# Where the weight-sum transfers of a two-layer hybrid transformer start, and which result each of them follows

## The chip, the cores and the metric

The kernel runs on one core of a Trainium2 chip. The metric is device time in microseconds (us) from launch to end, the median of several executions. The engines of a core work side by side, each through its own instructions in order: PE (TensorE) multiplies matrices, DVE (VectorE), ACT (ScalarE) and POOL (GpSimd) work on elements, SP (SyncE) does nothing here but issue DMA transfers. POOL issues some DMAs too. An instruction waits until what it reads has been written and what it overwrites has been read.

## The reference

Two layers of a transformer for 512 tokens of width 1024, in float32. Each layer is a half feed-forward network (width 2816), a token mix and another half feed-forward network, each with a residual and a layer norm:

```python
for l in range(DEPTH):
    x = _layer_norm(DN_ALPHA * x + 0.5 * _swiglu(x, ffn1_w1[l], ffn1_w2[l]), ln1_g[l], ln1_b[l])
    mix = _token_mix(x, w_in[l], ...)
    x = _layer_norm(DN_ALPHA * x + mix, ln2_g[l], ln2_b[l])
    x = _layer_norm(DN_ALPHA * x + 0.5 * _swiglu(x, ffn2_w1[l], ffn2_w2[l]), ln3_g[l], ln3_b[l])
```

The token mix projects the tokens with `w_in`, runs three kinds of attention over the parts, and merges them with gates:

```python
q_a, kv_a, g_a, q_b, k_b, v_b, q_c, k_c, v_c, f_c = _split_cols(h @ w_in)
o_a = _nsa(...)        # compressed, selected and windowed attention
o_b = _swa_sink(...)   # sliding window with sinks
o_c = _fox(...)        # attention with forget gates
g = jax.nn.sigmoid(h @ w_gate + b_gate).reshape(B, S, N_BRANCH, D)
merged = g[:, :, 0] * (o_a @ w_br_a) + g[:, :, 1] * (o_b @ w_br_b) + g[:, :, 2] * (o_c @ w_br_c)
return merged @ w_out
```

The first attention's compressed branch makes its keys and values by a small network over blocks of 32 tokens: `gelu(flat @ w1) @ w2`, with `cmp_k_w1`, `cmp_v_w1` (2048 x 256 each) as its first layer.

## The kernel before

**Matmuls.** Every large product is made of three matmuls of a reduced float type: a weight tile `raw` (128x1024, 512 KB) is loaded by SP, ACT rounds it to `hi` (L154), DVE makes `lo` = raw - hi (L155), and PE multiplies `hi` by the tokens' high and low part and `lo` by the high part (L175 to L177). `raw`, `hi` and `lo` have three buffers each, so the split of a tile waits until the tile three before it has been used by all that read it.

**The token mix** (`mix`) begins with 30 *chunks* (L1153 on), each a projection of 128 columns, split into 8 parts that are put between pieces of the attention. The chunks' weights are `w_in`, and `w_gate` for the last five. Among the first chunks PE also runs the cumulated forget gates (`cum`, L789 and L792) and, between parts, 16 steps of the compressed branch's first layer (`hid`, L842), whose weights are the 16 pairs of loads `cw` (L835, one pair for keys and values, 256 KB together). The `cw` tiles share the tag "p" and its 13 buffers with probabilities and other things, the `gl` tile of the forget gates among them, which `cum` reads. Behind the first layer comes `tr` (L855), run within the thirteenth chunk. Probabilities are normed (L915) on DVE or POOL and transposed by PE.

Behind the chunks comes the branches' part: for each of eight `d`, three gates (L1377 on; the result is `t`, with four buffers), the branch products `brp` with `oh` and `ol` (the split attention outputs, L1393 and L1394), and their sum `mh`. The branches' weights are `raw` of 256 KB each (L1371).

**Sums of weights.** The second layer of three of the four feed-forward networks is computed from sums of blocks of its weights (`ts`, in DRAM). They are made by DMA alone: `weight_sums` (L384) puts 24 steps for one weight into a queue, in three groups of eight. Each step is one transfer of 768 KB from DRAM to DRAM, issued by POOL (L396). Steps 3, 5, 6 and 7 of a group add onto what is there; steps 6 and 7 add sums onto sums (`ts<-ts`), and step 7 waits for step 6 to have landed. Layer 0 of `mix` has two weights to sum (48 steps), layer 1 has one (24). In all 72 steps.

One step is taken at the end of each chunk (L1167) and of each gate's matmuls (L1384), by `sums_step` (L402): POOL first copies one column of the `hi` tile that this chunk or gate uses to `pace`, then issues the transfer. The copy holds the transfer until that `hi` has been made, and it makes the copy one of the readers of `hi`.

**What sets the order.** PE and POOL run in the order in which the program is written; ACT, DVE and SP are ordered by a scheduler at build time.

Of the kernel before, what the change touches and what calls it, by code (L numbers as in the profile page):

```python
# [9 lines left out]
F32 = mybir.dt.float32  # L10
F32R = mybir.dt.float32r
BF = mybir.dt.bfloat16
AF = mybir.ActivationFunctionType
# [5 lines left out]
P = 128  # L19
S, D, F = 512, 1024, 2816  # L20
KD, KF, NB = D // P, F // P, S // P
# [43 lines left out]
def body(tc, a, out, depth=DEPTH):  # L65
    nc = tc.nc
    PE, POOL = mybir.EngineType.PE, mybir.EngineType.Pool

    def pool(name, bufs=1, side=None, **kw):
        return tc.alloc_tile_pool(name=name, bufs=bufs, side=side, **kw)  # L70

    const = pool("const")
# [8 lines left out]
    def ps(tag=None, name="ps", shape=(P, 512)):  # L81
        if tag is None:
            tag = PS_ALL[ring[0] % 8]
            ring[0] += 1
        return psp.tile(list(shape), F32, name=name, tag=tag, bufs=PS_TAGS[tag])
# [16 lines left out]
    bgate = const.tile([P, depth, 3, KD], F32, name="bgate")  # L102
    peT = const.tile([P, depth, 2, 32], F32, name="peT")
    stats = [const.tile([P, 8], F32, name=f"st{i}") for i in range(NB)]
    pace = const.tile([P, 48], F32, name="pace")[:, 0:1]

    xh = xtp.tile([P, KD, S], F32R, name="xh")
    xl = xtp.tile([P, KD, S], F32R, name="xl")
# [49 lines left out]
    def wcols(w, c0, step=None):  # L158

        r = wraw()  # L160
        nc.sync.dma_start(r, w.rearrange("(k p) f -> p k f", p=P)[:, :, c0:c0 + P])
        return wsplit(r, step=step)
# [16 lines left out]
    def proj(o, w, n=slice(0, S), ks=range(KD)):  # L179
        for k in ks:  # L180
            mm3(o[:, n], w, k, xh[:, k, n], xl[:, k, n], k == 0, k == KD - 1)
# [200 lines left out]
    sums = deque()  # L382
# [16 lines left out]
            sums.extend(lambda g=g, i=i: step(g, i) for i in range(8))  # L399
        return ts  # L400

    def sums_step(w, n=1):  # L402
        for _ in range(n):
            if sums:
                nc.gpsimd.tensor_copy(pace, w[0][:, KD - 1, 0:1].bitcast(F32))
                sums.popleft()()

    PLAIN = (0, 1, 2, 3)

# [245 lines left out]

    def mix(l, wts, pend, done_ffn, xap, xa, nxt):
        m = K()
        PB = 13
        w_in = a["w_in"][l]
        wb = [a["w_br_a"][l], a["w_br_b"][l], a["w_br_c"][l]]  # L660
# [91 lines left out]
        def ev_gf(p):  # L752
# [3 lines left out]
            def rest():  # L756
                pt = ps("tp", "gfT", (P, NB, 64))
                for tb in range(NB):
                    nc.tensor.transpose(pt[:, tb], t[0:64, tb * P:(tb + 1) * P], ident[0:64, 0:64])
                w = at.tile([P, 11, NB, H], F32, name="gl", tag="p", bufs=PB)  # L760
                gs = w[:, 0:4].rearrange("p a b h -> p (a b h)").rearrange("p (b c) -> p b c", b=NB)
# [41 lines left out]
        def ev_z(p, i):  # L803

            z = [at.tile([P, 8, 2, NSLOT], F32, name="z", tag="p", bufs=PB) for _ in range(2)]
            nc.gpsimd.memset(z[1][:, :, :, NSLOT - 1:NSLOT], 0.0)
# [13 lines left out]
        def conv(ws):  # L820


            c = K()
            w2 = at.tile([P, 2, 3, DH], F32, name="cw2", tag="p", bufs=PB)
            c.wk, c.wv = w2[:, :, 0:2], w2[:, :, 2]
            v = a["cmp_k_w2"][l].rearrange("(c p) d -> p c d", p=P)
            for r in range(2):
                nc.sync.dma_start(c.wk[:, :, r], v)
            nc.sync.dma_start(c.wv, a["cmp_v_w2"][l].rearrange("(c p) d -> p c d", p=P))
            wv = [w.rearrange("(c p) f -> p c f", p=P) for w in ws]  # L830

            def load(k):
                r = at.tile([P, 2, 256], F32, name="cw1", tag="p", bufs=PB)
                for i in range(2):
                    nc.sync.dma_start(r[:, i], wv[i][:, k])  # L835

                def go():
                    if k == 0:
                        c.p = ps("sc", "hid", (P, 256))
                    for i in range(2):  # L840
                        z = (m.zk, m.zv)[i][k // 8][:, k % 8].rearrange("p g n -> p (g n)")
                        nc.tensor.matmul(c.p[64 * i:64 * i + 64], z, r[:, i], start=k == 0, stop=k == 15)  # L842
                    if k == 15:
                        x = at.tile([P, 2, 256], F32, name="gl", tag="p", bufs=PB)
                        t, c.t = x[:, 0], x[:, 1]
                        nc.scalar.activation(t, c.p, AF.Square)
                        nc.vector.tensor_scalar(t, t, 0.044715, 1.0, op0=OP.mult, op1=OP.add)
                        nc.vector.tensor_tensor(t, t, c.p, op=OP.mult)
                        nc.scalar.activation(t, t, AF.Tanh, scale=GELU_C)
                        nc.vector.scalar_tensor_tensor(c.t, t, 1.0, c.p, op0=OP.add, op1=OP.mult)  # L850
                return go

            def tr():
                pt = ps("tp", "glT", (P, 2, P))
                for f in range(2):  # L855
                    nc.tensor.transpose(pt[:, f], c.t[:, f * P:(f + 1) * P], ident)
                x = at.tile([P, 3, P], F32, name="glt", tag="p", bufs=PB)
                c.gk = x[:, 0].rearrange("p (f n) -> p f n", f=2)
                c.gv = x[:, 1:3].rearrange("p f (g r n) -> p f g r n", g=2, r=2)
                nc.vector.tensor_copy(c.gk, pt[:, :, 0:64])  # L860
                for f in range(2):
                    nc.vector.tensor_copy(c.gv[:, f], pt[:, f, 64:P].rearrange("p (g n) -> p g n", g=2)[:, :, None]
                                          .to_broadcast([P, 2, 2, NSLOT]))

            c.n = 0

            def feed():

                if c.n < 16 and len(narrow) < 4:
                    narrow.append(load(c.n))  # L870
                    c.n += 1

            def end():
                while narrow or c.n < 16:
                    feed()
                    narrow.popleft()()
                tr()

            return c, feed, end
# [37 lines left out]
        class Swa:  # L917
            br, nseg, ngrp = 1, 1, 1
# [53 lines left out]
        class Fox:  # L972
            br, nseg, ngrp = 2, 2, 2
# [48 lines left out]
        class Nsa:  # L1022
            br, nseg = 0, 2
# [132 lines left out]
        def chunk(c0, then, w=w_in, load=wcols, bank="mm"):  # L1156
            st = K()

            def part(i):
                def go():  # L1160
                    if i == 0:
                        st.w = load(w, c0)
                        st.p = ps(bank, "pj")
                    proj(st.p, st.w, ks=range(i, i + 1))
                    if i == 7:
                        then(st.p)
                        sums_step(st.w)  # L1167
                return go

            fill.extend(part(i) for i in range(8))  # L1170
# [101 lines left out]
        def gate_ev(t, p, br, d):  # L1272
            nc.scalar.activation(t, p, AF.Tanh, scale=0.5, bias=bg[:, br, d:d + 1])
# [94 lines left out]
        def wbr(d, brs):  # L1368
            r = wraw()
            for j, br in enumerate(brs):  # L1370
                nc.sync.dma_start(r[:, 4 * j:4 * j + 4],  # L1371
                                  wb[br].rearrange("(k p) f -> p k f", p=P)[:, :, d * P:(d + 1) * P])
            return wsplit(r[:, 0:4 * len(brs)], 4 * len(brs))

        def gates(d):
            g_t = []
            for br in range(3):  # L1377
                if d == 1 and br < 2:
                    p = held[br]
                else:  # L1380
                    p = ps("sc" if d == 1 else None, "gate")
                    w = wcols(a["w_gate"][l], br * D + d * P)
                    proj(p, w)
                    sums_step(w)  # L1384
                t = tp_.tile([P, S], F32, name="t", tag="t", bufs=4)
                gate_ev(t, p, br, d)
                g_t.append(t)
            return g_t

        g_1 = gates(1)  # L1390
        for br in (1, 2, 0):
            for i in range(4):
                nc.scalar.activation(oh[br][i], o_t[br][i], AF.Copy)  # L1393
                nc.vector.tensor_tensor(ol[br][i], o_t[br][i], oh[br][i].bitcast(F32), op=OP.subtract)  # L1394
        for d in range(KD):
            g_t = gates0 if d == 0 else g_1 if d == 1 else gates(d)
            for br in (1, 2, 0):
                if br != 2:
                    w = wbr(d, (1, 2) if br else (0,))
                k0 = 4 if br == 2 else 0  # L1400
                p = ps(name="brp")
                for k in range(4):
                    mm3(p, w, k0 + k, oh[br][k], ol[br][k], k == 0, k == 3)
                t = g_t[br]
                nc.vector.scalar_tensor_tensor(t, t, 1.0, p, op0=OP.add, op1=OP.mult)
                if br != 1:
                    nc.vector.tensor_tensor(g_t[1], g_t[1], t, op=OP.add)
            nc.scalar.activation(mh[:, d], g_t[1], AF.Copy)
            nc.vector.tensor_tensor(ml[:, d], g_t[1], mh[:, d].bitcast(F32), op=OP.subtract)
# [147 lines left out]
```

## Time and profile before

| | us |
|---|---|
| median of the runs shown | 2498.09 |
| those three runs | 2498.33, 2498.09, 2495.55 |
| the profiled execution | 2495.75 |
| its span (first to last instruction) | 2494.0 |
| mean granted clock of PE | 0.993 |

| DMA issue | count | KB each | us to landing, median |
|---|---|---|---|
| `raw<-in_w_in_dram` | 56 | 512 | 5.0 |
| `raw<-in_w_gate_dram` | 48 | 512 | 5.3 |
| `ts<-in_ffn_w_dram` (steps 0 to 5) | 54 | 768 | 7.9 |
| `ts<-ts` (steps 6 and 7) | 18 | 768 | 8.8 |

A row of a timeline has the start in us, the duration (of several alike: the stretch), the engine and line, the operation with output and inputs, the count, and in brackets the idle time of that engine before it with what ended it. "SPq" and "POOLq" are rows of an engine's queue, DMA issues above all. A row of a table of stretches has the stretch, its length, the busy time of PE, PE's weight loads, DVE, ACT and POOL with the number of their instructions, and at its end the granted clock, the DMA engines' mean busy share and GB/s. The names in the rows are those of the program; `cw` is `cw1` in the code.

### The profile page before, as it was taken

How to read it: one execution, taken by the hardware profiler on the slowest of the kernel's cores; microseconds unless marked ns; L12 is line 12 of the kernel's file. 1: busy time of each engine (PE TensorE's matmuls, PEld its weight loads, DVE VectorE, ACT ScalarE, POOL GpSimd, SP SyncE). 2: the span in 40 equal slices, each digit the busy share in tenths (PEclk: the TensorE clock that was granted, in tenths of full speed). 3: DMA queues.
4: the chain of work that ended last, by engine and by line, in shares of the span. 5: the costliest groups of instructions: out<-in, count | busy, mean ns of one | idle time of the engine just before them, and what ended most of it. 6: DMA issues, size and time to landing. Idle time of an engine off the chain costs nothing. (4 is left out here: it accounts for less than half of the span.)

```text
span 2494.0 us, 40924 instructions
## 1 busy us (share of the span) xinstructions
PE 2443.8 (98%) x15529; PEld 2159.3 (87%) x15529; DVE 1763.2 (71%) x3554; ACT 1172.6 (47%) x2226; POOL 325.6 (13%) x598
## 2 busy tenths in 40 slices
PE   9999999899999999999999999979999999999998
PEld 8999887688878889999889998867888888899987
DVE  7888365477754367998879889655776543698887
ACT  4444334466642333445534446434766422344453
POOL 4000001234422100000000000112443000000000
PEclk9999999899999999999999999999999999999999
DMA  7445345885578642336623346668662433333463
GB/s 205 113 118 161 119 111 166 225 179 147 127 193 224 156 143 86 103 111 207 203 93 103 109 155 204 194 152 227 157 149 60 144 90 121 119 94 102 132 211 127
DMA packets 411460, 364.05 MB, mean 146 GB/s; under 512 B 19720, under 2 KB 351640, under 8 KB 411264
## 3 DMA queue, kind: packets, MB, share of 16 engines
q1 hardware_dynamic: 381968, 279.92, 38.0%
q0 software_dynamic: 29296, 81.53, 13.6%
q8 instruction: 122, 2.00, 0.3%
q14 instruction: 74, 0.61, 0.1%
HBM read 334.07 MB, written 74.51 MB: 164 GB/s over the span
## 5 line engine op out<-in xcount | busy, mean ns | idle before, releaser
L155 DVE TENSOR_TENSOR lo<-raw,hi 128x1024 fp32r<-128x1024 f32 (+2 forms) x384 | 450.5, 1182 | 379.3 <-ACT hi L154 374.5
L154 ACT ACTIVATE hi<-raw 128x1024 fp32r<-128x1024 f32 (+2 forms) x384 | 390.6, 1024 | 600.2 <-issue 149.9
L175 PE MATMUL pj<-xh,hi 128*128 128x512 f32 (+1 forms) x720 | 267.6, 372 | 0.2 <-ACT hi L154 0.2
L176 PE MATMUL pj<-xl,hi 128*128 128x512 f32 (+1 forms) x720 | 255.5, 355 | 1.1 <-DVE xl L241 1.1
L177 PE MATMUL pj<-xh,lo 128*128 128x512 f32 (+1 forms) x720 | 255.1, 354 | 0.0
L515 PE MATMUL pg<-xh,hi 128*128 128x256 f32 x864 | 245.1, 284 | 1.7 <-ACT sn L522 1.5
L515 PE MATMUL pg<-xh,lo 128*128 128x256 f32 x864 | 244.5, 283 | 0.0
L515 PE MATMUL pg<-xl,hi 128*128 128x256 f32 x864 | 244.5, 283 | 0.0
L435 ACT ACTIVATE hi<-ws 128x1024 fp32r<-128x1024 f32 x144 | 151.5, 1055 | 160.2 <-DVE ws L427 72.7
L436 DVE TENSOR_TENSOR lo<-ws,hi 128x1024 fp32r<-128x1024 f32 x144 | 175.4, 1220 | 17.6 <-ACT hi L435 17.4
L274 PE MATMUL acc<-hi,sh 128*128 128x512 f32 x450 | 175.5, 390 | 0.0
L274 PE MATMUL acc<-lo,sh 128*128 128x512 f32 x450 | 175.1, 389 | 0.0
L274 PE MATMUL acc<-hi,sl 128*128 128x512 f32 x450 | 175.1, 389 | 0.0
L515 PEld LDWEIGHTS pg<-xh,hi 128*128 128x128 f32 x864 | 165.8, 192 | 3.1 <-ACT sn L522 2.9
L515 PEld LDWEIGHTS pg<-xl,hi 128*128 128x128 f32 x864 | 165.8, 192 | 0.2
L515 PEld LDWEIGHTS pg<-xh,lo 128*128 128x128 f32 x864 | 165.8, 192 | 0.0
L515 PE MATMUL pu<-th,hi 128*128 128x256 f32 x576 | 163.0, 283 | 0.0
L515 PE MATMUL pu<-tl,hi 128*128 128x256 f32 x576 | 163.0, 283 | 0.0
L515 PE MATMUL pu<-th,lo 128*128 128x256 f32 x576 | 163.0, 283 | 0.0
L177 PEld LDWEIGHTS pj<-xh,lo 128*128 128x128 f32 x720 | 136.7, 190 | 19.8
L175 PEld LDWEIGHTS pj<-xh,hi 128*128 128x128 f32 x720 | 137.2, 191 | 15.5 <-issue 3.1
L176 PEld LDWEIGHTS pj<-xl,hi 128*128 128x128 f32 x720 | 137.3, 191 | 12.9 <-DVE xl L241 1.4
(365 smaller groups left out, 6251.4 us busy)
## 6 DMA issues: line engine op xcount, KB each, us to landing
raw<-in_ffn_w_dram SPq DMA_DIRECT2D x237, 512.0 KB, 4.0
ts<-in_ffn_w_dram POOLq DMA_DIRECT2D x54, 768.0 KB, 7.9
raw<-in_w_in_dram SPq DMA_DIRECT2D x56, 512.0 KB, 5.0
raw<-in_w_gate_dram SPq DMA_DIRECT2D x48, 512.0 KB, 5.3
raw<-ts SPq DMA_DIRECT2D x39, 512.0 KB, 4.1
ts<-ts POOLq DMA_DIRECT2D x18, 768.0 KB, 8.8
x_sp<-xa POOLq DMA_DIRECT2D x24, 512.0 KB, 6.1
ks<-hl SPq DMA_DIRECT2D x96, 128.0 KB, 4.9
```

The lines of the kernel that those rows point to most:

```text
L154: nc.scalar.activation(hi[:, c], raw[:, c], AF.Copy)
L155: nc.vector.tensor_tensor(lo[:, c], raw[:, c], hi[:, c].bitcast(F32), op=OP.subtract)
L175: nc.tensor.matmul(o, hi[:, k], vh, start=first, stop=False)
L176: nc.tensor.matmul(o, hi[:, k], vl, start=False, stop=False)
L177: nc.tensor.matmul(o, lo[:, k], vh, start=False, stop=last)
L274: nc.tensor.matmul(o, xx[:, t], ww[:, c], start=first and i == 0, stop=last and i == 2)
L435: nc.scalar.activation(hi, x, AF.Copy)
L436: tt(lo, x, hi.bitcast(F32), op=OP.subtract)
L515: nc.tensor.matmul(o, wx, vx, start=first and k == 0 and i == 0, stop=k == 3 and i == 2, skip_group_check=True)
```

## The change

```diff
-    pace = const.tile([P, 48], F32, name="pace")[:, 0:1]
+    pace = const.tile([P, 48], F32, name="pace")
+    pace, pace2 = pace[:, 0:1], pace[0:64, 16:17]
...
-    def sums_step(w, n=1):
-        for _ in range(n):
-            if sums:
-                nc.gpsimd.tensor_copy(pace, w[0][:, KD - 1, 0:1].bitcast(F32))
-                sums.popleft()()
+    def sums_step(t, psum=False):
+        if sums:
+            if psum:
+                nc.scalar.activation(pace2, t[0:64, 0:1], AF.Copy)
+                t = pace2
+            nc.gpsimd.tensor_copy(pace[0:64], t[0:64, 0:1])
+            sums.popleft()()
...
         m = K()
+        m.free = False
...
             def tr():
+                m.free = True
...
                     if i == 7:
                         then(st.p)
-                        sums_step(st.w)
+                        if m.free:
+                            sums_step(st.p, True)
...
                     proj(p, w)
-                    sums_step(w)
                 t = tp_.tile([P, S], F32, name="t", tag="t", bufs=4)
                 gate_ev(t, p, br, d)
+                if not (d == 1 and br < 2):
+                    sums_step(t)
...
                 nc.vector.scalar_tensor_tensor(t, t, 1.0, p, op0=OP.add, op1=OP.mult)
+                if br != 2:
+                    sums_step(t)
```

A chunk takes a step only once `tr` has run (`m.free`), so the first twelve take none. Its step is held by the chunk's result in PSUM instead of its weight: ACT copies 64x1 of it to `pace2`, POOL copies that, then issues the transfer. A gate's step is held by its result `t`, and two more steps in each `d` follow the branch products, held by `t` too. POOL no longer reads `hi`.

The steps of layer 0 now are: 18 in chunks 13 to 30, one with the third gate of `d` 1 (which runs ahead of the loop), two in `d` 0, two in `d` 1 and five in each of `d` 2 to 6. In layer 1: 18 in chunks, one, two, two, and one in `d` 2.

*POOL, from the last rows before the attention's first norm of layer 0 on.* (`ts` is a transfer of a sum, `p` a probability tile, `tri` the triangle for `cum`, `z` the blocks for `hid`.) Before:

```order
L396 DMA ts<-in_ffn_w_dram 128x3x512
L405 COPY pace<-hi 128x1
L396 DMA ts<-in_ffn_w_dram 128x3x512
L782 AFFINE_SELECT tri<-ones 128x128
L915 TENSOR_SCALAR p<-p,stS 128x128 x2
L915 TENSOR_SCALAR p<-p,stS 128x256
L806 MEMSET z 128x16
L405 COPY pace<-hi 128x1
L396 DMA ts<-in_ffn_w_dram 128x3x512
```

The same place after:

```order
L669 DMA x_sp<-xa_2909 128x1024
L786 AFFINE_SELECT tri<-ones 128x128
L920 TENSOR_SCALAR p<-p,stS 128x128 x2
L920 TENSOR_SCALAR p<-p,stS 128x256
L810 MEMSET z 128x16 x2
L920 TENSOR_SCALAR p<-p,stS 128x256 x3
```

The copies and transfers among the norms are gone; the first pair now stands behind `vbd`, which is written when the first layer is done:

```order
L920 TENSOR_SCALAR p<-p,stS 128x128 x2
L920 TENSOR_SCALAR p<-p,stS 128x256 x4
L888 MEMSET vbd 128x256
L408 COPY pace<-pace 64x1
L397 DMA ts<-in_ffn_w_dram 128x3x512
```

*SP around the first four pairs of `cw` in layer 0* (`tab` is a table of position biases, `ncd` the forget gates' sums on their way through DRAM). Before (the fourth pair is 4297):

```order
L161 DMA raw_4566<-in_w_in_dram 128x8x128
L835 DMA cw1_4262<-in_cmp_k_w1_dram 128x256
L835 DMA cw1_4262<-in_cmp_v_w1_dram 128x256
L835 DMA cw1_4275<-in_cmp_k_w1_dram 128x256
L835 DMA cw1_4275<-in_cmp_v_w1_dram 128x256
L835 DMA cw1_4291<-in_cmp_k_w1_dram 128x256
L835 DMA cw1_4291<-in_cmp_v_w1_dram 128x256
L161 DMA raw_4698<-in_w_in_dram 128x8x128
L685 DMA tab_4853<-bvec_93 128x2x256
L161 DMA raw_4818<-in_w_in_dram 128x8x128
L835 DMA cw1_4297<-in_cmp_k_w1_dram 128x256
L835 DMA cw1_4297<-in_cmp_v_w1_dram 128x256
```

And now (the fourth pair is 4285):

```order
L162 DMA raw_4548<-in_w_in_dram 128x8x128
L162 DMA raw_4678<-in_w_in_dram 128x8x128
L839 DMA cw1_4250<-in_cmp_k_w1_dram 128x256
L839 DMA cw1_4250<-in_cmp_v_w1_dram 128x256
L839 DMA cw1_4263<-in_cmp_k_w1_dram 128x256
L839 DMA cw1_4263<-in_cmp_v_w1_dram 128x256
L839 DMA cw1_4279<-in_cmp_k_w1_dram 128x256
L839 DMA cw1_4279<-in_cmp_v_w1_dram 128x256
L689 DMA tab_4831<-bvec_93 128x2x256
L162 DMA raw_4796<-in_w_in_dram 128x8x128
L839 DMA cw1_4285<-in_cmp_k_w1_dram 128x256
L839 DMA cw1_4285<-in_cmp_v_w1_dram 128x256
```

One `raw` has moved from between the third and fourth pair to ahead of the first; the `raw` right ahead of the fourth pair is still the same chunk's.

*POOL behind the chunks of layer 0.* Before, one copy and one transfer for each gate, all copies of `hi`. Now:

```order
L408 COPY pace<-pace 64x1
L397 DMA ts<-in_ffn_w_dram 128x3x512
L408 COPY pace<-t 64x1
L397 DMA ts<-in_ffn_w_dram 128x3x512
L408 COPY pace<-g_4078 64x1
L397 DMA ts<-in_ffn_w_dram 128x3x512
L408 COPY pace<-g_4077 64x1
L397 DMA ts<-in_ffn_w_dram 128x3x512
L408 COPY pace<-t 64x1
```

The first copy is that of the last chunk, the second that of the gate ahead of the loop, the two of `g` those of `d` 0 (its gates are chunks, so that only the products give steps). From there on each copy reads a `t`.

## The prediction

> **What bounds the kernel now.** I read the page first, then the waits of the matrix engine (PE), then its timeline around the longest wait, then backwards, engine by engine, to what that wait hangs on.
>
> ```profile
> PE 2443.8 (98%) x15529; PEld 2159.3 (87%) x15529; DVE 1763.2 (71%) x3554; ACT 1172.6 (47%) x2226; POOL 325.6 (13%) x598
> ...
> PE hid L842 <- DMA cw<-in_cmp_k_w_dram: 26.2, 2, 13.5
> ...
> PE brp L175 <- ACT oh L1393: 2.2, 1, 2.2
> ...
> PE brp L175 <- DVE g L1405: 1.2, 1, 1.2
> ...
> PE brp L177 <- DVE lo L155: 0.4, 1, 0.4
> ...
> PE brp L176 <- DVE ol L1394: 0.2, 1, 0.2
> ```
>
> The first row is from the busy table; the others are PE's waits (total, times, longest). PE is busy for 98% of the span and the order of its work stays as it was, so the change can win only where PE stands still or runs at a lower clock. Of the 50 us without PE work (2494.0 - 2443.8), 26.2 us are two waits, one in each layer, of the compressed branch's first layer (`hid`) for its weights (`cw`). The timeline of PE shows them, layer 0 first, then layer 1:
>
> ```profile
> 432.23 0.38 PE L789 MATMUL cum<-tri,gl 128*8 128x128 f32 x2
> ...
> 433.25 1.47 PE L842 MATMUL hid<-cw,z 128*64 128x256 f32 x12
> 447.44 1.53 PE L842 MATMUL hid<-cw,z 128*64 128x256 f32 x4 [12.73 <-DMA cw<-in_cmp_k_w_dram]
> ...
> 450.78 0.63 PE L175 MATMUL pj<-xh,hi 128*128 128x512 f32 x1
> ...
> 453.30 0.40 PE L175 MATMUL pj<-xh,hi 128*128 128x512 f32 x1
> ...
> 1681.12 1.51 PE L842 MATMUL hid<-cw,z 128*64 128x256 f32 x4 [13.49 <-DMA cw<-in_cmp_k_w_dram]
> ...
> 1685.59 0.40 PE L175 MATMUL pj<-xh,hi 128*128 128x512 f32 x1
> ```
>
> Three of the first four pairs of `cw` are there (12 matmuls), the fourth is not. And PE does not resume at full speed: the same matmul takes 0.63 us before 453.30 and 0.40 from there on, and in layer 1 it is back at 0.40 by 1685.59. The table of stretches grants half a clock meanwhile (its last three numbers are clock, DMA share, GB/s):
>
> ```profile
> 444.00:448.00 4.00, 0.56 (x3) 0.42 (x4) 0.00 (x0) 0.00 (x0) 0.00 (x0) 0.50 1.12 296
> ```
>
> At half speed, 447.44 to 453.30 loses 5.9 / 2 = 2.9 us, and 1681.12 to 1685.59 loses 4.5 / 2 = 2.2 us. The chain behind the late `cw`, in the timelines of POOL, ACT, DVE and SP's queue:
>
> ```profile
> 430.74 0.56 POOL L915 TENSOR_SCALAR p<-p,stS 128x256 f32<-128x256 f32 x1 [8.56 <-ACT p L947]
> ...
> 433.45 0.18 POOL L405 COPY pace<-hi 128x1 f32<-128x1 f32 x1
> 433.58 1.23 POOL L396 DMA_DIRECT2D ts<-in_ffn_w_dram  x1
> ...
> 434.50 2.69 POOL L396 DMA_DIRECT2D ts<-ts  x1
> ...
> 433.67 1.06 ACT L154 ACTIVATE hi<-raw 128x1024 fp32r<-128x1024 f32 x1 [1.74 <-POOL pace L405]
> ...
> 434.75 1.23 DVE L155 TENSOR_TENSOR lo<-raw,hi 128x1024 fp32r<-128x1024 f32 x1 [2.35 <-ACT hi L154]
> ...
> 436.01 0.37 SPq L161 DMA_DIRECT2D raw<-in_w_in_dram  x1
> 436.47 0.87 SPq L835 DMA_DIRECT2D cw<-in_cmp_k_w_dram  x1
> 437.39 0.50 SPq L835 DMA_DIRECT2D cw<-in_cmp_v_w_dram  x1
> ```
>
> POOL had sat for 8.56 us before a norm, so its copy that reads a `hi` tile ran only at 433.45. ACT may not overwrite that buffer before; the split ends at 434.75 + 1.23 = 435.98; the next `raw` leaves at 436.01, and the fourth pair of `cw` stands right behind it in SP's queue. Then it is slow to land. The DMA issues of 430 to 440, and below them those of 461 to 466, where no sum runs (count, KB, median us to landing):
>
> ```profile
> ts<-ts POOLq DMA_DIRECT2D x1, 768.0 KB, 11.8
> cw<-in_cmp_k_w_dram SPq DMA_DIRECT2D x1, 128.0 KB, 10.9
> ...
> cw<-in_cmp_k_w_dram SPq DMA_DIRECT2D x4, 128.0 KB, 4.3
> ```
>
> So the stall has two parents: a late issue (436.47), and two sums transfers beside the load (10.9 us against 4.3).
>
> **The change part by part.** *No sums before the thirteenth chunk.* This takes 12 pace copies and 12 transfers in each layer out of the stretch in which `hid` runs, and with them both parents. What is late next? In SP's order the fourth pair still stands behind a `raw`, but that one now hangs on a split that waits for PE alone. The pair then needs a buffer of the tag "p" that PE's last `cum` matmul reads until 432.23 + 0.38 = 432.6. The first of the pair leaves at 432.6, the second 0.9 us behind it (437.39 against 436.47), landing takes some 4 us: about 437.3, and PE wants it at 433.25 + 1.47 = 434.7. I take 2.6 us a layer as what is left of 12.73 and 13.49 (ends 1.5, for a landing a quarter quicker, and 6, for one half as contended as before), and 0.5 for the following groups of `hid`.
>
> *The clock after the stall.* Whether 2.6 us drop it is open. The nearest row is the tail below, where four gaps of 2.17, 0.23, 1.22 and 0.41 us were enough to halve it. I take half of the measured loss (mean of 2.9 and 2.2), 1.3 us a layer, with ends 0 and 2.9. The Trainium skill ("TensorE: Matmul & The Clock Gate", section "HAM oscillation — how this bites in real kernels") warns only of gaps of PE over about 3.4 us; by it this gap would cost no clock, and the forecast would be 2.6 us lower. The row at 719.80 below, at 0.63 us with no gap that long near it, speaks against it.
>
> *The tail of layer 0.* The branches' weights stall PE once more:
>
> ```profile
> 693.36 0.18 POOL L405 COPY pace<-hi 128x1 f32<-128x1 f32 x1
> ...
> 693.57 1.06 ACT L154 ACTIVATE hi<-raw 128x1024 fp32r<-128x1024 f32 x1 [0.56 <-POOL pace L405]
> ...
> 695.92 0.37 SPq L1371 DMA_DIRECT2D raw<-in_w_br_a_dram  x1
> ...
> 707.61 0.63 ACT L154 ACTIVATE hi<-raw 128x512 fp32r<-128x512 f32 x1 [8.93 <-DMA raw<-in_w_br_a_dram]
> ...
> 710.29 0.49 PE L175 MATMUL brp<-oh,hi 128*128 128x512 f32 x1 [2.17 <-ACT oh L1393]
> ...
> 719.80 0.63 PE L177 MATMUL brp<-oh,lo 128*128 128x512 f32 x1
> ...
> 722.78 0.44 PE L175 MATMUL brp<-oh,hi 128*128 128x512 f32 x1
> ```
>
> Again ACT's split waits for a pace copy, a 256 KB load leaves late into a burst of sums, and arrives 11.7 us later (707.61 - 695.92). PE's idle is 2.17 + 0.23 + 1.22 + 0.41 = 4.0 us, and half a clock from about 719.4 to 722.8 loses 1.6: together 5.6. With `hi` bound to PE alone the load leaves before that burst, and ACT has 8.93 us of idle in hand. I count the 5.6 as won (ends 0 and 5.6).
>
> *36 small copies on ACT, wait for wait on POOL.* ACT is busy for 47%, and these are among the shortest things it does; nothing of it shows on PE. ACT now waits for POOL's last copy before it writes `pace2` again, and DVE's product waits for the copy that reads `t`. What stands behind POOL's copies are norms, for which PE's transposes wait. But a POOL that sits 8.56 us before a norm comes to most copies when PE's result has long been there. Ends 0 and 5 us; I take 0.
>
> *Sums moved into the branches' loop.* In layer 0 five for each `d` from 2 to 6, where there were three; in layer 1, where there were none, six behind chunk 30. The page's queues (packets, MB, share of the 16 engines' span), the gate's loads and one stretch of that loop, and two issues one `d` apart:
>
> ```profile
> q1 hardware_dynamic: 381968, 279.92, 38.0%
> q0 software_dynamic: 29296, 81.53, 13.6%
> ...
> 740.00:760.00 20.00, 20.00 (x90) 16.57 (x89) 9.89 (x12) 6.93 (x9) 5.44 (x6) 1.00 0.94 257
> ...
> raw<-in_w_gate_dram SPq DMA_DIRECT2D x13, 512.0 KB, 5.3
> ...
> 763.42 0.37 SPq L1371 DMA_DIRECT2D raw<-in_w_br_b_dram  x1
> ...
> 787.78 0.37 SPq L1371 DMA_DIRECT2D raw<-in_w_br_b_dram  x1
> ```
>
> One sum takes 0.136 x 2494 / 81.53 x 0.786 MB = 3.3 us of all engines; the weights of one `d` (2.36 MB) take 0.38 x 2494 / 279.92 x 2.36 = 8.0. Five sums and the weights are 24.4 us in a `d` of 24.4 us (787.78 - 763.42). That is a share of 1.0, against 0.94 at 740 to 760, where PE is busy for all 20.00 us. It just fits; I take 2 us for it (ends 0 and 30, the latter worked out below).
>
> **The sum**, against the profiled execution's own 2495.75 us: 12.73 + 2.9 + 13.49 + 2.2 + 5.6 = 36.9 us could go. Left are 2 x (2.6 + 0.5 + 1.3) = 8.8, and 2 are new: 26 won, **2470 us**. The median of the runs shown is 2498.09, 2.3 above that execution, so against it the win would be 28.
>
> **The rivals.** *The stall only shrinks.* If the fourth pair leaves no sooner than, say, 436, for another wait in front of it on SP (its `raw`, say, or the slower norms), only the contention goes: it lands at 441, 6 us late, and the clock still halves. Then about 2 x (6 + 2.5 + 0.5) = 18 of 31.3 stay: 2495.75 - 13.3 - 3 = 2480, up to 2488 without the tail's gain. For it speaks that eight transfers of `cw` and three other loads share one queue; against it, that its `raw` hangs on nothing slow any more.
>
> *Nothing that can be measured.* The fourth pair waits as long for something else, or the transfers that are put off come together with later weights and PE loses there what it won: 2493 to 2498. Also the case in which the pace copies go but the late norms turn out to hold `raw` themselves. Against it speaks that ACT's row at 433.67 names POOL's copy and not a norm.
>
> *Slower.* In the loop over `d` the queues are full, a gate's load takes 11 us instead of 5.3, like `cw` did beside two sums, and each `d` ends some 6 us later: five times 6 are 30 us, 2470 + 30 = 2500. It decides as soon as each `d` loses over 5 us. Besides, POOL is held there by the step that adds onto a sum still under way (`ts<-ts`, 11.8 us), and DVE waits for its copy. Against it stands the share of 0.94 that PE bore without idle.
>
> *The clock holds* through what is left of the stall: 2.6 us less, 2467.
>
> **How the numbers follow.** A measurement of this kernel tells about 0.2%, 5 us, from no change. Forecast 0.52, clock holds 0.18, the stall only shrinks 0.16, nothing 0.07, slower 0.07. Faster is the first three, 0.86. The range goes from 2460, where all but a stall of 1.5 us in each layer is won (36.9 - 3 gives 2462, and 2 for the run's own spread), to 2490, the end of the stall that only shrinks; what is left out are the last two cases.
>
> **What would show it.** PE's waits: `hid` at 2 to 4 us a layer instead of 12.73 and 13.49, and no waits of `brp`. SP's queue: the fourth pair at 432 to 434, relative to `cum`. DMA issues: `cw` near 4 us to landing. No split of ACT waits for POOL. The granted clock behind `hid` tells the first forecast from the one in which it holds. Wrong would be: `hid` waits on `cw` for over 6 us, or new waits of PE for `hi`, `lo` or `t` in the loop over `d`, or a DMA share at 1.1 there with loads of 10 us.

## The result and the profile after

| | before | after |
|---|---|---|
| median of four runs, us | 2498.21 | 2471.57 |
| those runs, us | 2495.55 to 2499.05 | 2469.47 to 2472.68 |
| ratio, with 95% interval | | 0.9894 [0.9877, 0.9911] |
| span of the profiled execution, us | 2494.0 | 2470.9 |
| mean granted clock of PE | 0.993 | 0.997 |

The kernel is 26.6 us faster (2498.21 - 2471.57), and the measured median lies 1.6 us above the forecast of 2470. The page's busy table of the changed kernel:

```profile
PE 2443.8 (99%) x15529; PEld 2157.1 (87%) x15529; DVE 1763.6 (71%) x3554; ACT 1171.5 (47%) x2262; POOL 328.0 (13%) x598
```

PE's waits of the changed kernel (total, times, longest):

```profile
PE xT L1506 <- DMA xa<-in_x_dram: 4.6, 1, 4.6
PE ptN L1117 <- DVE pc L703: 3.0, 2, 1.5
PE ptN L1117 <- ACT p L705: 2.0, 2, 1.0
...
PE gate L176 <- ACT hi L155: 1.4, 1, 1.4
```

PE's busy time is the same to a tenth of a microsecond, so the two spans differ by idle time alone. That hides the clock: the matmuls at half clock behind `hid` are gone, but this execution had a lower clock early on (below), and the two come out about even. The 26.2 us of `hid` are no longer in the list, and new, smaller waits are: of transposes (`ptN`) and of gates. Around the fourth pair of `cw` (L839 now), from the timelines of PE and of SP's queue:

```profile
435.20 0.38 PE L793 MATMUL cum<-tri,gl 128*8 128x128 f32 x2
...
436.22 2.69 PE L846 MATMUL hid<-cw,z 128*64 128x256 f32 x16
438.84 1.18 PE L939 MATMUL sS<-ks,qs 128*128 128x128 f32 x8
439.86 0.40 PE L176 MATMUL pj<-xh,hi 128*128 128x512 f32 x1
...
435.61 0.34 SPq L839 DMA_DIRECT2D cw<-in_cmp_k_w_dram  x1
```

The DMA issues of 435 to 440 have its landing:

```profile
cw<-in_cmp_k_w_dram SPq DMA_DIRECT2D x1, 128.0 KB, 2.1
```

`cum` ends at 435.58, the pair leaves at 435.61 as forecast, lands in 2.1 us, and all 16 matmuls of `hid` run as one group, with the full clock (0.40) behind them.

**Where the time went.** PE runs the same 15529 matmuls in the same order in every kernel here. So the start of each matmul in one trace can be set against the start of the same matmul in the trace of before, and the change of that difference over a stretch is what the stretch lost (+) or won (-). The stretches are those of before, in us: start 0 to 425, first layer of the compressed branch (425 to 510, 1640 to 1760), chunks (510 to 700, 1760 to 1925), the tail where branch products begin (700 to 735, 1925 to 1990), the loop over `d` of layer 0 (735 to 910), the rest of layer 0 (910 to 1640), and the end (from 1990). The last column is the shift of the last matmul; it differs by up to 0.3 from the sum of its row, by rounding and by where the first matmul stands.

```
                start   hid0 chunk0  tail0   loop   rest   hid1 chunk1  tail1    end     sum
after            +2.7  -15.1   +1.8   -6.7   +7.3   +1.0  -16.3   +2.2   -0.0   -0.0   -23.1
early_psum       +4.4   -5.1   +1.8   -6.7   +0.7   -0.0  -10.6   +2.5   -0.0   +0.0   -13.3
late_copy        +0.4   -8.1   +2.0   -6.7   +4.8   +0.5   -9.3   +2.4   -0.0   +0.0   -13.8
late_hi          -0.6  -15.1   +0.7   -6.7   +7.2   -0.1  -16.2   +0.1   +1.1   +0.0   -29.5
tail_burst       +2.8  -15.1   +1.0   -4.4   -0.0   +0.4  -16.3   -0.2   +3.4   -0.0   -28.5
tail_step6       +2.2  -15.0   +1.0   -1.1   +0.0   -0.6  -16.3   +0.0   +3.1   -0.0   -26.7
four_per_d       +3.1  -15.2   +1.6   -6.7   +1.0   -0.1  -16.3   +2.8   -0.0   +0.0   -29.9
two_in_chunks    +1.8  -15.1   +3.1   -6.7   +0.0   -0.1  -16.4   +2.7   -0.0   +0.0   -30.7
hi_two           +1.7  -15.1   +5.0   -4.2   -0.0   -0.3  -16.3   +0.0   +1.6   +0.1   -27.7
hi_four          -0.9  -15.1   +0.7   -6.7   +1.3   +3.1  -16.1   -0.0   +1.5   +0.1   -32.2
hi_two_early     +1.6  -15.1   +1.1   -6.7   +0.0   -0.4  -15.6   -0.0   +1.1   -0.0   -34.2
```

The first row is the change; the others are the experiments. The change wins 31.4 us at `hid` (15.1 + 16.3) and 6.7 in the tail, and gives back 7.3 in the loop, 4.0 in the chunks and 1.0 behind the loop: 25.8 won. The first column, up to 4.4 us, comes from before 370 us, ahead of every edit; most of it arises from 20 to 60 us, where the profiled executions differ by the granted clock (0.93 and 0.90 in the profile after, 1.00 before), so the table compares better than the spans do. Each row is one execution. How far such a row can be trusted shows in `late_copy`, which has the changed kernel's code from the thirteenth chunk on and yet loses 4.8 in the loop, not 7.3.

### The profile page after: what moved, and what is told of

Its sections match the earlier page's. It is cut to its first block, busy times and chain, and to the rows that moved or that the text cites. A ratio compares the mean times of both kernels' runs of the same rounds, so it can differ in the third digit from the quotient of the medians.

```text
span 2470.9 us, 41023 instructions
## 1 busy us (share of the span) xinstructions
PE 2443.8 (99%) x15529; PEld 2157.1 (87%) x15529; DVE 1763.6 (71%) x3554; ACT 1171.5 (47%) x2262; POOL 328.0 (13%) x598
```

## The experiments

Each kernel is told by its edit against the changed kernel. Medians are of four runs, with the ratio to the kernel before, run beside them.

**Two parents of the stall, one at a time.** `early_psum` takes the late start away and keeps the new hold, so that sums run beside `cw`, but POOL does not read `hi`:

```diff
-                        if m.free:
-                            sums_step(st.p, True)
+                        sums_step(st.p, True)
```

> The new hold (the chunk's result) without the late start: every chunk takes a step from the first on, and hi is free of POOL. If the late issue of the fourth pair of cw alone made the stall, hid waits under 1 us and the time is at or under the changed kernel's 2471, since fewer sums are left for the loop over d. If the sums beside the load make it as well, the pair leaves right behind cum but lands in 8 to 11 us, hid waits 5 to 8 us a layer, the clock halves, and the time is 2478 to 2488.

2484.74 us, 0.9944 [0.9928, 0.9961]. (One of its four runs took 6684 us and is left out of the ratio; the others lie at 2479 to 2487.) From the timelines of PE and of SP's queue around the fourth pair:

```profile
441.59 0.65 PE L846 MATMUL hid<-cw,z 128*64 128x256 f32 x2 [2.11 <-DMA cw<-in_cmp_k_w_dram]
443.56 0.81 PE L846 MATMUL hid<-cw,z 128*64 128x256 f32 x2 [1.33 <-DMA cw<-in_cmp_v_w_dram]
...
437.33 0.34 SPq L839 DMA_DIRECT2D cw<-in_cmp_k_w_dram  x1
```

And its DMA issues of 437 to 438.5:

```profile
cw<-in_cmp_k_w_dram SPq DMA_DIRECT2D x1, 128.0 KB, 4.2
cw<-in_cmp_v_w_dram SPq DMA_DIRECT2D x1, 128.0 KB, 5.8
```

The landing is 4.2 and 5.8 us against 2.1, about half of what was expected. It is not the sum issued next to the pair (at 437.10) that slows its first part: from 437 to 440 all the packets that the DMA engines moved are of SP's queue (packets, MB, share of the 16 engines).

```profile
q1 hardware_dynamic: 1513, 1.01, 111.6%
```

The pair shares the engines with SP's own loads, which the two sums before it (issued at 424.81 and 426.11) had held up: the `raw` that left at 426.15 took 10.5 us to land. How sums hold up loads can be seen in the kernel before, from 442 to 444, when its sums run beside `cw`, and below that from 447 to 448, when they are done (queue 0 has POOL's transfers, queue 1 SP's):

```profile
q0 software_dynamic: 164, 0.34, 90.2%
q1 hardware_dynamic: 164, 0.08, 21.0%
...
q1 hardware_dynamic: 657, 0.34, 115.3%
```

Both queues move the same number of packets, 164 each in 2 us, but those of the sums are four times as large. So SP's loads get 0.04 MB per us in place of 0.34. In `early_psum` later groups of `hid` wait too, and the clock drops again, so that 10.0 of the 15.1 us come back in layer 0 and 5.7 of 16.3 in layer 1.

`late_copy` is the other half: in the first twelve chunks POOL copies a column of `hi`, as it did before, and issues nothing.

```diff
                         if m.free:
                             sums_step(st.p, True)
+                        else:
+                            nc.gpsimd.tensor_copy(pace[0:64], st.w[0][0:64, KD - 1, 0:1].bitcast(F32))
```

> As the change, but in the first twelve chunks of each layer POOL still copies a column of the chunk's hi tile, as before the change, and issues no transfer: the late issue alone, without sums beside the load. If the late issue counts by itself, the fourth pair of cw leaves some 4 us behind the end of cum and lands in about 4 us; hid waits 4 to 7 us a layer, and the time is 2480 to 2488. If only the transfers beside it count, hid waits under 1 us and the time is that of the changed kernel, 2471.

2482.06 us, 0.9940 [0.9925, 0.9955]. From the timelines of ACT, SP's queue and PE:

```profile
434.29 2.00 ACT L155 ACTIVATE hi<-raw 128x1024 fp32r<-128x1024 f32 x2 [1.73 <-POOL pace L1175]
...
437.11 0.53 SPq L839 DMA_DIRECT2D cw<-in_cmp_k_w_dram  x1
...
440.95 1.51 PE L846 MATMUL hid<-cw,z 128*64 128x256 f32 x4 [5.57 <-DMA cw<-in_cmp_k_w_dram]
...
444.27 0.63 PE L176 MATMUL pj<-xh,hi 128*128 128x512 f32 x1
```

And its DMA issues of 436 to 438.2:

```profile
cw<-in_cmp_k_w_dram SPq DMA_DIRECT2D x1, 128.0 KB, 3.8
```

The chain of before is back without any sum: POOL's copy is late, the split waits for it, the pair leaves at 437.11 instead of behind `cum`, and even with a landing of 3.8 us (a `raw` left 0.48 us ahead of it) PE stands for 5.57 us and resumes at half clock. That is 7.0 us of 15.1 in layer 0 and 7.0 of 16.3 in layer 1. Both parents are real; together (10.0 + 7.0, 5.7 + 7.0) they make up the 15.1 and 16.3 within 2 to 4 us.

**The hold in the chunks.** `late_hi` keeps the late start and lets the chunks' copies read `hi` again:

```diff
-                nc.scalar.activation(pace2, t[0:64, 0:1], AF.Copy)
-                t = pace2
+                t = t[0][:, KD - 1].bitcast(F32)
...
-                            sums_step(st.p, True)
+                            sums_step(st.w, True)
```

> The late start of the change is kept; in the chunks POOL's copy reads the chunk's hi tile again, so that ACT's next split waits for POOL as before. If the tail's stall in layer 0 came from hi being tied to POOL, it returns here: waits of brp of 2 to 4 us and some 5 to 7 us from 687 to 725, a time of 2474 to 2480. If it came from the number of sums at that place alone, it stays away, and the time is that of the changed kernel, 2471. In both cases the wait of hid is under 1 us in each layer, since no sum runs there. If ACT's changed order costs the 1.9 and 2.2 us that PE lost in the later chunks, these come back as a gain.

2467.14 us, 0.9883 [0.9868, 0.9897]. The tail's stall stays away although the split waits for POOL again; the chunks lose 0.7 and 0.1 us in place of 1.8 and 2.2. What the chunks had lost shows in the changed kernel's timelines at 597 (PE, then DVE):

```profile
597.65 0.52 PE L1117 MATMUL ptN<-ident,p 128*128 128x128 f32 x3 [1.49 <-DVE pc L703]
...
595.59 1.22 DVE L156 TENSOR_TENSOR lo<-raw,hi 128x1024 fp32r<-128x1024 f32 x1
...
597.22 0.29 DVE L703 COPY pc<-ptC 128x128 f32<-128x128 f32 x1
```

A split that is free of POOL has been put ahead of the copy that empties PE's bank, and the transposes wait for it. In `late_hi` DVE runs the same split behind that copy:

```profile
593.58 0.29 DVE L702 COPY pc<-ptC 128x128 f32<-128x128 f32 x1
...
598.59 1.29 DVE L156 TENSOR_TENSOR lo<-raw,hi 128x1024 fp32r<-128x1024 f32 x1 [0.56 <-ACT hi L155]
```

All kernels here whose chunks are held by PSUM have this wait of 1.5 us in each layer; none of those held by `hi` has it. It is an order that the scheduler chose at build, and not the time that ACT's 36 copies take.

**What made the tail's stall.** `tail_burst` is `late_hi` with the third gate's step of `d` 1 held by its weight and put ahead of the gate's result, as before the change:

```diff
+                if d == 1 and br == 2:
+                    sums_step(w, True)
                 gate_ev(t, p, br, d)
-                if not (d == 1 and br < 2):
+                if d != 1:
                     sums_step(t)
```

> As the kernel with late start and hi copies in the chunks (2467), but the step of the third gate of d 1 follows its hi tile again, ahead of the gate's result, in both layers: three sums in a burst beside the load of the first branch weight. If the third transfer made the tail's stall, it comes back: PE waits for oh and the branch products' operands, 2 to 4 us and a half clock behind it in each layer, 2471 to 2478. If something else of the change removed it, the time stays at 2467.

2466.60 us, 0.9872 [0.9855, 0.9888]. The last step of the burst, the load and ACT's split of it, first in `late_hi`, where the burst has two steps (timelines of POOL, SP's queue, ACT):

```profile
679.56 0.78 POOL L397 DMA_DIRECT2D ts<-in_ffn_w_dram  x1
...
681.08 0.37 SPq L1376 DMA_DIRECT2D raw<-in_w_br_a_dram  x1
...
687.48 0.63 ACT L155 ACTIVATE hi<-raw 128x512 fp32r<-128x512 f32 x1 [3.68 <-DMA raw<-in_w_br_a_dram]
```

The same in `tail_burst`, where it has three:

```profile
684.49 0.73 POOL L397 DMA_DIRECT2D ts<-in_ffn_w_dram  x1
...
684.53 0.37 SPq L1376 DMA_DIRECT2D raw<-in_w_br_a_dram  x1
...
693.42 0.63 ACT L155 ACTIVATE hi<-raw 128x512 fp32r<-128x512 f32 x1 [6.15 <-DMA raw<-in_w_br_a_dram]
```

From issue to split it is 6.4 us (687.48 - 681.08) with two, 8.9 with three. The tail loses 2.3 of the 6.7 us in layer 0, and in layer 1, where before no sum ran at that place, 3.4 (1.1 in `late_hi`). The time does not rise, since the loop over `d` loses nothing now (below). In `tail_burst` the three are steps 0 to 2 of a group, of which none adds. Before the change they were steps 4 to 6: the second adds onto what is there, the third adds sums onto sums (`ts<-ts`). `tail_step6` takes two steps in four early chunks, so that they are steps 4 to 6 again:

```diff
                             sums_step(st.w, True)
+                            m.two += 1
+                            if l == 0 and m.two <= 4:
+                                sums_step(st.w, True)
```

> The kernel with the third gate's step ahead of the gate's result, with two steps in each of the first four chunks that take any in layer 0, so that the third transfer of the burst beside the first branch weight is one that adds sums onto sums, as it was before the change. There the third transfer of the plain kind gave back 2.3 of the 6.7 us that the change won at that place. If the kind of the third step makes up the rest, PE loses there about 6 to 7 us against the changed kernel; if not, 2 to 3 us again. The whole time is 2464 to 2471 either way, since the loop over d takes back what PE loses ahead of it.

2470.74 us, 0.9902 [0.9885, 0.9918]. The timelines of POOL, SP's queue, ACT and PE:

```profile
682.69 1.28 POOL L397 DMA_DIRECT2D ts<-in_ffn_w_dram  x1
...
684.15 1.22 POOL L397 DMA_DIRECT2D ts<-ts  x1
...
684.20 0.37 SPq L1379 DMA_DIRECT2D raw<-in_w_br_a_dram  x1
...
696.41 0.63 ACT L155 ACTIVATE hi<-raw 128x512 fp32r<-128x512 f32 x1 [9.45 <-PE gate L178]
...
699.10 0.49 PE L176 MATMUL brp<-oh,hi 128*128 128x512 f32 x1 [2.69 <-ACT oh L1404]
```

12.2 us from issue to split, PE's wait for `oh` is back at 2.69 (2.17 before), and the tail loses 5.6 of its 6.7 us (-1.1 in the table). (The row names a gate's matmul as the releaser, which ended at the same moment; in the two kernels above the same split ran while that gate was still going.) So three steps at one place, the second and third of them adding, made this stall; how much of it each of the two makes was not separated.

In the changed kernel itself the load does not stand behind the burst at all (timelines of SP's queue, POOL, ACT):

```profile
682.69 0.37 SPq L1377 DMA_DIRECT2D raw<-in_w_br_a_dram  x1
...
684.50 0.80 POOL L397 DMA_DIRECT2D ts<-in_ffn_w_dram  x1
...
688.60 0.63 ACT L155 ACTIVATE hi<-raw 128x512 fp32r<-128x512 f32 x1 [0.51 <-PE pj L177]
```

With `hi` free of POOL it leaves 1.8 us ahead of the first sum, and ACT's split no longer waits for it. So the changed kernel has two remedies. `late_hi` shows that the shorter burst alone is enough in layer 0, while it loses 1.1 us in layer 1, where the changed kernel loses nothing. Whether the freed `hi` alone would be enough beside three steps was not run.

**The rate in the loop over `d`.** `four_per_d` drops one of the two steps behind the products from `d` 3 on, and so goes on to the last `d`; `two_in_chunks` drops both from `d` 2 on and takes two steps in every second chunk instead:

```diff
-                if br != 2:
+                if br == 1 or br == 0 and d < 3:
                     sums_step(t)
```

```diff
                             sums_step(st.p, True)
+                            m.two += 1
+                            if l == 0 and m.two % 2 == 0:
+                                sums_step(st.p, True)
...
-                if br != 2:
+                if br != 2 and d < 2:
                     sums_step(t)
```

> As the change, but of the two steps behind the branch products only one is kept from d 3 on, so that layer 0 has four steps per d up to the last d in place of five up to d 6. If the 7.2 us that PE lost there come from the rate of the sums against the weights (a share of 1.0), the loss falls to 2 to 3 us: 2466 to 2468. If it comes from DVE and ACT waiting for POOL's copies, most of it stays: 2470 to 2472.

> As the change, but in layer 0 every second chunk from the thirteenth on takes two steps, and the branch products take none from d 2 on: nine sums more in the chunks, three per d in the loop as before the change. If the rate in the loop is the price, it falls to under 1 us there: 2464 to 2467. If sums cost PE wherever they run beside weights, the chunks lose what the loop wins: 2470 to 2473.

2466.41 us, 0.9880 [0.9863, 0.9896], and 2465.24, 0.9872 [0.9857, 0.9886]. The loop loses 1.0 and 0.0 us in place of 7.3; the two steps in every second chunk cost 1.3 in the chunks (3.1 against 1.8). In the changed kernel PE's timeline in the loop, and below it the split of ACT that it waits for, look like this:

```profile
819.82 0.50 PE L176 MATMUL gate<-xh,hi 128*128 128x512 f32 x1 [1.38 <-ACT hi L155]
820.16 0.39 PE L177 MATMUL gate<-xl,hi 128*128 128x512 f32 x1
821.08 0.50 PE L178 MATMUL gate<-xh,lo 128*128 128x512 f32 x1 [0.53 <-DVE lo L156]
...
822.57 0.63 PE L177 MATMUL gate<-xl,hi 128*128 128x512 f32 x1
...
825.54 0.40 PE L178 MATMUL gate<-xh,lo 128*128 128x512 f32 x1
...
818.71 1.06 ACT L155 ACTIVATE hi<-raw 128x1024 fp32r<-128x1024 f32 x1 [12.64 <-DMA raw<-in_w_gate_dram]
```

Its stretch of 120 us in that loop (busy times, and at the end clock, DMA share, GB/s):

```profile
723.00:843.00 120.00, 117.42 (x507) 95.66 (x506) 42.22 (x50) 34.79 (x45) 30.41 (x44) 0.99 0.96 249
```

Its gate loads among the DMA issues of 700 to 860:

```profile
raw<-in_w_gate_dram SPq DMA_DIRECT2D x17, 512.0 KB, 13.1
```

The same two views of `two_in_chunks`, with three steps per `d`, the stretch first:

```profile
723.00:843.00 120.00, 120.00 (x531) 99.37 (x530) 47.68 (x56) 37.56 (x48) 22.71 (x31) 1.00 0.91 237
```

And its gate loads:

```profile
raw<-in_w_gate_dram SPq DMA_DIRECT2D x17, 512.0 KB, 5.4
```

A gate's weight takes 13.1 us to land instead of 5.4, ACT's split waits for it and PE for the split, and the clock halves for 3 us. The other explanation, waits for POOL's copies, had 2470 to 2472 for four steps; it was 2466.41, and ACT's row names the load and no copy.

Five steps per `d`, and loads as late as these, need not cost anything, though: `tail_burst` has as many steps as `late_hi` and loses 0.0 against 7.2. Its stretch and its gate loads:

```profile
723.00:843.00 120.00, 120.00 (x531) 99.38 (x530) 45.92 (x55) 35.22 (x45) 33.88 (x49) 1.00 1.00 256
...
raw<-in_w_gate_dram SPq DMA_DIRECT2D x17, 512.0 KB, 13.1
```

So neither the number of steps, nor the share, nor the median landing tells what PE loses. `tail_burst` comes to the loop 2.6 us later than `late_hi` (0.3 in the chunks, 2.3 in the tail), with the gate's step already on its way ahead of it. Which of the two frees the loop was not tried. What is shown is that fewer steps there save most of the loss, and that some order of the same steps does too; why is open.

**Together.** `hi_two` is `late_hi` with the edit of `two_in_chunks`, `hi_two_early` the same with the doubled steps in the first eight chunks that take any (`m.two <= 8`), `hi_four` is `late_hi` with the edit of `four_per_d`.

> The two that did better than the change put together: hi copies in the chunks with the late start, two steps in every second chunk of layer 0, none behind the branch products from d 2 on. If the gains add (4 us in the chunks, 6 in the loop over d), 2460 to 2463. If the hi copies of twice as many steps hold ACT's splits, 2464 to 2468.

> Hi copies in the chunks with the late start, two steps in each of the first eight chunks that take any in layer 0 (so none doubled near the tail), none behind the branch products from d 2 on. If the tail's stall of the kernel with doubled steps up to the last chunk (3 us) came from a third sum in the burst, it is gone here, and the loop has three per d: 2460 to 2464. If doubled steps hold PE in the chunks, as by 3 us there, 2463 to 2467.

> Hi copies in the chunks with the late start (2467) and four steps per d up to the last d (2466): no third sum beside the first branch weight, and the loop over d under a share of 1.0. If the two gains add, 4 us and 6 us off the changed kernel's 2471: 2460 to 2463. If the loop only takes back what PE wins ahead of it, because there the transfers set the pace, 2465 to 2467.

`hi_two`: 2467.34 us, 0.9881 [0.9867, 0.9896]: a step doubled in the last chunk makes a burst of three at the tail (-4.2 in place of -6.7), and the chunks lose 5.0. `hi_two_early`: 2463.47, 0.9867 [0.9852, 0.9881], with the tail's 6.7 and the loop whole. `hi_four`: 2463.88, 0.9864 [0.9848, 0.9881], with 1.3 lost in the loop and 3.1 behind it. The last two have lower medians than both kernels, by about 8 us against the changed one; but their intervals overlap that of the change and each other.

## Why the prediction was right

*Right by its mechanism:* the two waits of `hid` were the prize, their two parents (the late issue and the sums beside the load) were each shown by an experiment that leaves only one (in `early_psum` the sums act through the loads ahead of the pair as well), and the fourth pair now leaves at the end of `cum`, as it said.

*Too large:* what is left of the stall. I took 2.6 us a layer, 0.5 for later groups and 1.3 for the clock, 8.8 in all; the `hid` stretches won 31.4 us against the 31.3 (12.73 + 2.9 + 13.49 + 2.2) that could go, so nothing is left. The landing had been taken as 4 us, from a place where four pairs and a `raw` shared the queue (4.3); with no load left ahead of it the pair took 2.1. The question of the clock never arose.

*Too small:* the loop over `d`, 2 us against 7.3. The share of 1.0 was worked out, and then read as "just fits"; in the changed kernel loads of 13.1 us and a halved clock show that it does not. The reckoning also falls short of what is measured: for the three steps of before it gives (3 x 3.3 + 8.0) / 24.4 = 0.73, where 723 to 843 of that kernel has a share of 0.87. One of the signs that were named for being wrong came true, new waits of PE for `hi` and `lo` in the loop, and half of another: loads of over 10 us, at a share of 0.96 and not 1.1. The waits cost less than the rest won. The rival that called it slower had the mechanism (gate loads of 11 us), not the size: it reckoned 6 us for each of five `d`, and the whole loop lost about that once. Left out altogether were the chunks, 4.0 us from a build order that the new hold changed.

*The tail:* 5.6 us forecast, 6.7 measured, with a reason that is only half of it. The load does leave ahead of the burst, as forecast. But `late_hi` has `hi` tied and no stall in layer 0: that the gate's new hold takes the third step out of the burst and puts it behind the gate is enough there by itself (`tail_burst`, `tail_step6`), and the prediction did not see it.

So 26 us forecast and 25.8 measured along PE's matmuls are close by luck, with errors against each other: 8.8 us of stall that was not left, and 5.3 + 4.0 + 1.0 of new waits in the loop, the chunks and behind the loop, less 1.1 more won in the tail. The upper end of the range, 2490, rests on 2488 for the stall that only shrinks; the terms given for it come to 2480 with the tail's gain and some 2484 without (2495.75 - 13.3 + 2), so that end was not worked out.

*The clock.* The Trainium skill ("TensorE: Matmul & The Clock Gate", section "HAM oscillation — how this bites in real kernels") tells of idle gaps over about 3.4 us; at 819 to 822 gaps of 1.38 and 0.53 us halved it. As in the tail of before, the trace does not agree with that as a lower limit.

## What to carry to other kernels

When a side task is held by a tile of the main path, its copy is a reader of that tile, and a late copy on another engine holds the main path: hold it by something that nobody waits to overwrite. Moving background transfers away from a stall is not free: reckon the share of the place where they go. Here a measured share of 0.96 to 1.00 came with loads that land two to three times later, at a price of 0 to 7 us, depending on the kernel. Look at what several transfers at one place do to the one small load that is needed next, and compare packets of the queues, not only bytes.

## What was not expected of the hardware

Beside transfers with larger packets, a queue of loads falls far behind: in the kernel before both queues moved 164 packets in 2 us, and the loads got 0.04 MB per us in place of 0.34. Three steps ahead of a small load held it up longer when two of them add: 8.9 us from issue to split with steps 0 to 2, 12.2 with steps 4 to 6. And a delay ahead of the loop did not add to the loss in it: `tail_burst` enters the loop 2.6 us later than `late_hi` and leaves it 4.6 us sooner (7.2 - 2.6).
